# A first norm by channel without transposes, its output kept once

## The chip, the core and the metric

The kernel runs on one core of a Trainium2 chip. The core has five engines that run on their own and wait for each other by semaphores: TensorE (PE; its weight loads are PEld), VectorE (DVE), ScalarE (ACT), GpSimd (POOL) and SyncE (SP), which here only issues DMA transfers. ScalarE and GpSimd issue transfers too. Sixteen DMA engines carry them out. The time is that of the device, in microseconds; a lower one is better.

## What is computed

One layer of a diffusion trunk over 2048 sample tokens and 128 prompt tokens, in float32. Only its beginning matters here:

```python
mod = (jax.nn.silu(cond) @ w_ada + b_ada)[..., None, :]
shift1, scale1, gate1, shift2, scale2, gate2 = jnp.split(mod, 6, axis=-1)
h = rmsnorm(x, g_mix) * (1 + scale1) + shift1
p = h @ w_in
qkv, z, a_raw, b_raw, f = jnp.split(p, IN_SPLITS, axis=-1)
qkv = jax.nn.silu(short_conv(qkv, w_conv)).astype(jnp.float32)
```

`rmsnorm` divides each token's 1024 values by their root mean square. What follows (a delta rule in chunks with triangular inverses, a Fourier group, the output projection, a second norm and a feed-forward part) is the same in both kernels.

## The kernel before

Products of nearly full float32 precision are made of three matmuls: each operand is split into a rounded part `hi` (a ScalarE copy into the matmul's format) and the rest `lo` (a VectorE subtraction), and hi·hi, hi·lo and lo·hi are added in PSUM. The method `split` does this for weights and activations.

The modulation columns come first: `mod_columns(0, ...)` loads 32 pieces of `w_ada`, splits and multiplies them. Beside them `load_halves(wk, 512)` loads and splits the keys' half of `w_in`; eight pieces of its columns for gates and Fourier part, `wfh` and `wfl`, come next.

Then `phase_a` goes over 17 tiles of 128 tokens, the prompt (t = 16) first. A tile is loaded with tokens on partitions; `norm` sums its squares (ScalarE), takes the power -0.5 on GpSimd and scales (ScalarE, `xn`); `norm_T` transposes its eight pieces on TensorE into PSUM and applies scale and shift, half on VectorE, half on ScalarE, into `h` with channels on partitions; two splits make `hi` and `lo`. Both are written to `hT` in DRAM, and 48 matmuls with `wfh` and `wfl` give gates (`ab`) and Fourier input (`f`). Between the tiles, further weights are split and the first block's `hb` loaded.

`qk_pass` then reads `hT` back in eight blocks of 256 tokens (`load_h`, tiles `hb`; the first block has the prompt's 128 columns too), and makes eight projections per block with convolution, activation, products of pairs and, by `fill`, pieces of the triangular inverses. `v_pass` reads all blocks again for values and z.

Each engine executes its instructions in a fixed order, which a scheduler sets when the program is built; the pools of tiles (`bufs`) decide when a load may begin. SyncE's queue issues most loads in one order, so one that waits holds those behind it.

Of the kernel before, what the change touches and what calls it, by code (L numbers as in the profile page):

```python
# [93 lines left out]
class K:  # L94
# [94 lines left out]
    def setup(self):  # L189
# [26 lines left out]
        self.hT = d([2, P, KT, N], F32, name="hT")  # L216
# [139 lines left out]

    def phase_a(self, wk):
# [3 lines left out]
        with ExitStack() as ctx:  # L361
# [8 lines left out]
            qk = self.load_halves(wk, 512)  # L370
            for i, _ in enumerate(self.mod_columns(0, tiles(), "m")):
                if i % 8 == 4:
                    next(qk)
# [7 lines left out]
            qk = chain(qk, self.load_halves(wq, 0))  # L381
            for n, t in enumerate([16] + list(range(16))):
                rows = slice(t * P, (t + 1) * P)
                x = work.tile([P, D], F32, tag="x", name="x")
                nc.sync.dma_start(x, A["x"][rows])
                hi = work.tile([P, KT, P], F32R, tag="hi", name="hi")
                lo = work.tile([P, KT, P], F32R, tag="lo", name="lo")
                self.norm_T(*self.norm(x, 0, work), 0, int(t == 16), hi, lo)
                nc.scalar.dma_start(self.hT[0, :, :, rows], hi.bitcast(F32))
                nc.gpsimd.dma_start(self.hT[1, :, :, rows], lo.bitcast(F32))  # L390
                f = work.tile([P, 512], F32, tag="f", name="f")
                for a, b in ((0, 264), (264, FW)):
                    ps = self.bank("acc")
                    for k in range(KT):
                        self.mm(ps[:, :b - a], hi[:, k], wh[k][:, a:b], start=(k == 0), stop=False)
                        self.mm(ps[:, :b - a], hi[:, k], wl[k][:, a:b], start=False, stop=False)
                        self.mm(ps[:, :b - a], lo[:, k], wh[k][:, a:b], start=False, stop=(k == KT - 1))
                    if a == 0:
                        nc.vector.tensor_copy(self.ab[:, t], ps[:, :16])
# [99 lines left out]
    def load_h(self, n):  # L499
# [10 lines left out]
        tiles = []  # L510
        for k in range(KT):
            if n == 0:
                pair = []
                for l in range(2):
                    t = self.hb.tile([P, BW + NP], F32R, tag="hb", name="hb")
                    nc.sync.dma_start(t.bitcast(F32)[:, :BW], self.hT[l, :, k, start:start + BW])
                    nc.sync.dma_start(t.bitcast(F32)[:, BW:], self.hT[l, :, k, NS:])
                    pair.append(t)
                tiles.append(pair)
                continue  # L520
            t = self.hb.tile([P, 2, BW], F32R, tag="hb", name="hb")
            nc.sync.dma_start(t.bitcast(F32), self.hT[:, :, k, start:start + BW].rearrange("l p t -> p l t"))
            tiles.append((t[:, 0], t[:, 1]))
# [28 lines left out]
    def qk_pass(self, work, wq, wk, ahead):  # L552
        nc, sets, setp = self.nc, self.sets, self.setp
        late = deque()
        for n, b in enumerate(ORDER):
# [17 lines left out]
            for i, (q, h2, which) in enumerate(order):  # L573
# [228 lines left out]
    def v_pass(self, work, wv, wz, ahead):  # L802
# [3 lines left out]
        for n in [7] + list(range(7)):  # L806
# [665 lines left out]
def host_arrays(i):  # L1472
    f = lambda a: np.ascontiguousarray(a)
    a = {k: np.asarray(v) for k, v in i.items()}
    return {
        "x": f(np.concatenate([a["x_sample"][0], a["x_prompt"][0]], 0)),
# [32 lines left out]
```

## Time and profile before

| | |
|---|---|
| median of three runs | 2730.36 us (2729.53 to 2742.19) |
| the profiled execution | 2734.04 us, span 2732.3 us |
| TensorE, its weight loads | 96%, 87% of the span |
| VectorE, ScalarE, GpSimd | 66%, 51%, 11% of the span |
| TensorE's granted clock | 0.982 of full, mean |
| read from memory, written | 294.74 MB, 98.79 MB |

The span runs from the first to the last instruction; busy shares are means over stages with different limits. Lines such as L131 are mostly those of helpers, so instructions are told apart by their tiles: `lo<-h,hi` is the subtraction of a token tile, `w_in<-w_raw,w_in` that of a weight, `hb<-hT` a block's load.

### The profile page before, as it was taken

The numbers are of one execution on the slowest core, as the hardware profiler recorded it, in microseconds if no ns is written. First come the engines' busy times: TensorE is split into PE (matmuls) and PEld (weight loads), VectorE is DVE, ScalarE is ACT, GpSimd is POOL, SyncE is SP. The second block draws the span as 40 slices with busy tenths as digits, with TensorE's granted clock in tenths as the row PEclk, the third lists the DMA queues.
The fourth block names the chain that finished last, engine by engine and source line by source line (L and its number), as shares of the span: only waits on it lengthen the run. The fifth ranks groups of instructions, "written<-read, shape, count | busy, mean of one in ns | idle before, by whom it ended". The sixth has DMA issues, their size and how long they took to land.

```text
span 2732.3 us, 44881 instructions
## 1 busy us (share of the span) xinstructions
PE 2612.4 (96%) x15769; PEld 2374.1 (87%) x15769; DVE 1799.2 (66%) x3916; ACT 1404.5 (51%) x3108; POOL 312.5 (11%) x510
## 2 busy tenths in 40 slices
PE   6999999899999999997999999999999999999998
PEld 3898888799888778876999998889999888999986
DVE  6335978718256676667777766487776557888744
ACT  7756656323378877675333344444334444444432
POOL 1212222222300021211000000020000002000001
PEclk8999999999999999999999999999999999999999
DMA  9957768675666566645222223442222254323242
GB/s 314 307 152 222 222 192 233 185 197 177 159 182 194 174 190 183 184 143 170 78 74 70 74 82 122 140 128 74 73 71 72 88 159 138 90 85 89 90 135 93
DMA packets 436110, 396.50 MB, mean 145 GB/s; under 512 B 123084, under 2 KB 359164, under 8 KB 434284
## 3 DMA queue, kind: packets, MB, share of 16 engines
q1 hardware_dynamic: 345132, 297.65, 36.4%
q0 software_dynamic: 16624, 55.85, 6.2%
q10 hardware_dynamic: 74128, 40.13, 5.2%
q8 instruction: 125, 2.05, 0.3%
q14 instruction: 101, 0.83, 0.1%
HBM read 294.74 MB, written 98.79 MB: 144 GB/s over the span
## 4 chain that ended last, share of the span: by engine, by line
PE 58%; issue 15%; DMA 9%; DVE 8%; ACT 7%; POOL 2%; SPq 1%; ACTq 0%; DVEq 0%; POOLq 0%
PE acc L125 22%; PE m L125 12%; PE acc L1308 12%; PE m L1308 11%; DMA z_s<-z_d 1%; ACT h L141 1%; ACT bd1r L141 1%; PE tr L128 1%; ACT bd0r L141 1%; DMA w_raw<-w_ada 1%; PE tr L125 1%; ACT u L141 1%; DVE inv_d L131 1%; DMA a_d<-la 1%; POOL rstd L131 1%
## 5 line engine op out<-in xcount | busy, mean ns | idle before, releaser
L1308 PE MATMUL m<-h,wh 128*128 128x384 f32 (+1 forms) x1848 | 452.0, 327 | 5.3 <-ACT h L141 2.4
L1308 PE MATMUL acc<-h,wh 128*128 128x384 f32 (+1 forms) x1848 | 450.7, 327 | 2.0 <-ACT wh L141 2.0
L141 ACT ACTIVATE wh<-S 128x512 fp32r<-128x512 f32 x264 | 163.3, 630 | 377.9 <-DVE S L131 151.4
L1308 PEld LDWEIGHTS m<-h,wh 128*128 128x128 f32 x1848 | 327.0, 189 | 7.6 <-DVE U L131 2.9
L1308 PEld LDWEIGHTS acc<-h,wh 128*128 128x128 f32 x1848 | 326.8, 189 | 3.8 <-ACT wh L141 3.3
L125 PE MATMUL acc<-hb,w_in 128*128 128x258 f32 (+1 forms) x2304 | 324.6, 298 | 2.8 <-ACT conv_in L141 2.8
L125 PEld LDWEIGHTS acc<-hb,w_in 128*128 128x128 f32 x2304 | 312.5, 196 | 11.8 <-ACT conv_in L141 3.9
L1308 PE MATMUL acc<-h,wl 128*128 128x384 f32 (+1 forms) x924 | 300.9, 327 | 5.5 <-DVE wl L131 5.5
L1308 PE MATMUL m<-h,wl 128*128 128x384 f32 (+1 forms) x924 | 301.1, 327 | 0.0
L131 DVE TENSOR_TENSOR wl<-S,wh 128x512 fp32r<-128x512 f32 x264 | 178.7, 686 | 7.2 <-ACT wh L141 4.9
L141 ACT ACTIVATE wh<-w_gu 128x512 fp32r<-128x512 f32 x198 | 124.4, 631 | 113.3 <-issue 44.2
L1308 PEld LDWEIGHTS acc<-h,wl 128*128 128x128 f32 x924 | 174.2, 189 | 6.1 <-DVE wl L131 6.1
L1308 PEld LDWEIGHTS m<-h,wl 128*128 128x128 f32 x924 | 173.9, 188 | 0.2 <-DVE wl L131 0.2
L138 DVE SCALAR_TENSOR_TENSOR y<-conv_in,wconv,y 128x256 f32<-128x256 f32 (+1 forms) x216 | 97.7, 466 | 109.3 <-ACT conv_in L141 108.0
L141 ACT ACTIVATE awh<-a 128x384 fp32r<-128x384 f32 x176 | 91.3, 521 | 145.8 <-PE m L125 91.8
L131 DVE TENSOR_TENSOR awl<-a,awh 128x384 fp32r<-128x384 f32 x176 | 97.2, 555 | 97.4 <-ACT awh L141 96.7
L131 DVE TENSOR_TENSOR wl<-w_gu,wh 128x512 fp32r<-128x512 f32 x198 | 135.3, 685 | 24.8 <-ACT wh L141 24.6
L131 DVE TENSOR_TENSOR S<-w_gu 128x512 f32<-128x512 f32 x132 | 91.1, 691 | 84.8 <-DMA w_gu<-w_gu 84.3
L1424 POOL DMA_DIRECT2D half_d<-gy x17 | 9.3, 546 | 1148.6 <-DVE gy L131 1147.4
L138 DVE SCALAR_TENSOR_TENSOR r<-m,nsr,pk 64x128 f32<-64x128 f32 x272 | 94.7, 348 | 49.6 <-PE m L125 45.7
L125 PE MATMUL acc<-woh,mh 128*128 128x512 f32 x272 | 112.2, 413 | 1.5 <-DVE gx L131 1.4
L125 PE MATMUL acc<-wol,mh 128*128 128x512 f32 x272 | 109.3, 402 | 0.0
(295 smaller groups left out, 5780.6 us busy)
## 6 DMA issues: line engine op xcount, KB each, us to landing
w_gu<-w_gu SPq DMA_DIRECT2D x264, 256.0 KB
pk<-pk_d SPq DMA_DIRECT2D x68, 512.0 KB
w_dn<-w_down SPq DMA_DIRECT2D x132, 256.0 KB
hb<-hT SPq DMA_DIRECT2D x104, 258.0 KB
w_raw<-w_ada SPq DMA_DIRECT2D x32, 512.0 KB
x<-x SPq DMA_DIRECT2D x17, 512.0 KB
hT<-hi ACTq DMA_DIRECT2D x17, 512.0 KB
hT<-lo POOLq DMA_DIRECT2D x17, 512.0 KB, 6.1
```

What stands on the lines that cost most here:

```text
L125: self.nc.tensor.matmul(out, lhsT=lhsT, rhs=rhs, start=start, stop=stop)
L128: self.nc.tensor.transpose(out=out, in_=in_, identity=self.c("ident")[:in_.shape[0], :in_.shape[0]])
L131: (eng or self.nc.vector).tensor_tensor(out=out, in0=a, in1=b, op=op)
L138: self.nc.vector.scalar_tensor_tensor(out=out, in0=a, scalar=s, in1=b, op0=op0, op1=op1)
L141: self.nc.scalar.activation(out=out, in_=in_, func=f, **kw)
L1308: nc.tensor.matmul(o, lhsT=w_[:, ws], rhs=h_[:, k, :sub], start=start and k == i == 0, stop=k == 3 and i == 2, skip_group_check=not start)
L1424: nc.gpsimd.dma_start(self.half_d[n], tmp)
```

## The change

The host passes `xT`, x with channels on partitions. A token's sum of squares is now a sum over partitions: ScalarE squares, GpSimd adds the upper four pieces to the lower, VectorE adds twice, and a matmul with a column of ones ends the sum with tokens on partitions. VectorE takes mean and epsilon, GpSimd the power; VectorE puts the factors on a diagonal, a matmul of ones with it repeats them over all partitions, and VectorE multiplies x by that from PSUM. Scale and shift read SBUF. These five stages (`prepare`) run for three tiles at a time. `hT` keeps `h` once, in float32; `load_h` loads it into the tile for `lo`, and `split_h` makes `hi` and `lo` there, a few tiles per projection of the block before. The keys' weights are loaded between the token tiles, not in the modulation stage.

```diff
+    def col_sum(self, work, x):
+        sq = work.tile([P, KT, P], F32, tag="h", name="sq", bufs=3)
+        self.act(sq.rearrange("p k t -> p (k t)"), x.rearrange("p k t -> p (k t)"), AF.Square)
+        self.tt(sq[:, :4], sq[:, :4], sq[:, 4:], ALU.add, eng=self.nc.gpsimd)
+        self.tt(sq[:, :2], sq[:, :2], sq[:, 2:4], ALU.add)
+        total = work.tile([P, P], F32, tag="total", name="total")
+        self.tt(total, sq[:, 0], sq[:, 1], ALU.add)
+        return total
+    def col_factor(self, work, total):
+        ps = self.bank("tr")
+        self.mm(ps[:, 0:1], total, self.c("ones")[:, 0:1])
+        r = self.small.tile([P, 1], F32, tag="rstd", name="rstd", bufs=4)
+        self.ts(r, ps[:, 0:1], 1.0 / D, ALU.mult, EPS, ALU.add)
+        self.rsqrt(r, r)
+        dg = work.tile([P, P], F32, tag="dg", name="dg")
+        self.ts(dg, self.c("ident"), r, ALU.mult)
+        return ps, dg
+    def col_scale(self, x, ps, dg):
+        self.mm(ps[:, P:2 * P], self.c("ones"), dg)
+        self.tt(x, x, ps[:, P:2 * P].unsqueeze(1).to_broadcast([P, KT, P]), ALU.mult)
...
+        self.nc.scalar.dma_start(self.hT[:, :, rows], h)
...
+    def split_h(self, ahead, count):
+        tiles, _, width = ahead
+        for _ in range(count):
+            if self.whole:
+                hi, lo = (x[:, :width] for x in tiles[self.whole.popleft()])
+                self.act(hi, lo.bitcast(F32))
+                self.tt(lo, lo.bitcast(F32), hi.bitcast(F32), ALU.subtract)
...
+            first = {14: [(0, 0)], 18: [(1, 0)], 22: [(0, 1)], 24: [(0, 2), (1, 1)], 26: [(0, 3), (1, 2)], 28: [(1, 3)]}
             for i, _ in enumerate(self.mod_columns(0, tiles(), "m")):
-                if i % 8 == 4:
-                    next(qk)
+                for step in first.get(i, ()):
+                    prepare(*step)
...
-            qk = chain(qk, self.load_halves(wq, 0))
-            for n, t in enumerate([16] + list(range(16))):
+            qk = chain(self.load_halves(wk, 512), self.load_halves(wq, 0))
+            prepare(0, 4)
+            prepare(2, 0)
+            prepare(2, 1)
+            for n, t in enumerate(order):
...
-                self.norm_T(*self.norm(x, 0, work), 0, int(t == 16), hi, lo)
-                nc.scalar.dma_start(self.hT[0, :, :, rows], hi.bitcast(F32))
-                nc.gpsimd.dma_start(self.hT[1, :, :, rows], lo.bitcast(F32))
+                hi, lo = parts.pop(n)
+                prepare(n + 1, 4)
+                prepare(n + 3, 0)
...
+                prepare(n + 2, 3)
+                prepare(n + 3, 1)
-                if n >= 4:
+                if n % 2 == 0:
                     next(qk, None)
                 if n == 8:
                     ahead = self.load_h(0)
+                if n > 10:
+                    self.split_h(ahead, 2)
...
+                if n < 7 and i:
+                    self.split_h(ahead, 1 if i < 7 else 2)
...
+                if n != 6:
+                    self.split_h(ahead, 2)
```

VectorE's order before, up to the fifth token tile, to which `h_905` and `lo_904` belong (`h_813` and `lo_812` are the fourth's; `w_in` and `w_ada` are buffers with weights):

```order
L131 TENSOR_TENSOR w_in_482<-w_raw_1189,w_in_474 128x512
L135 TENSOR_SCALAR h_813<-tr_833,mod_cols_83 128x128 x2
L131 TENSOR_TENSOR w_in_483<-w_raw_1287,w_in_475 128x512
L131 TENSOR_TENSOR w_in_484<-w_raw_1287,w_in_476 128x512
L399 COPY ab_138<-acc_755 128x16
L131 TENSOR_TENSOR w_ada_2352<-w_raw_2351,w_ada_2352 128x512
L131 TENSOR_TENSOR w_ada_2395<-w_raw_2351,w_ada_2395 128x512
L135 TENSOR_SCALAR h_905<-tr_914,mod_cols_83 128x128 x2
L131 TENSOR_TENSOR lo_812<-h_813,hi_811 128x512
L135 TENSOR_SCALAR h_905<-tr_925,mod_cols_83 128x128 x2
L131 TENSOR_TENSOR lo_812<-h_813,hi_811 128x512
L131 TENSOR_TENSOR lo_904<-h_905,hi_903 128x512 x2
```

After the change the fifth tile is `x_677`, `h_843`, `lo_845`. Its `h_843` stands four rows ahead of the first row shown here, behind the scaling of `x_677` and weights of keys and queries; the rows lead to the second half of its `lo_845`:

```order
L131 TENSOR_TENSOR hb_1394<-hb_1394,hb_1393 128x386
L131 TENSOR_TENSOR hb_1398<-hb_1398,hb_1397 128x386
L131 TENSOR_TENSOR x_765<-x_765,tr_887 128x1024
L131 TENSOR_TENSOR hb_1402<-hb_1402,hb_1401 128x386
L131 TENSOR_TENSOR hb_1406<-hb_1406,hb_1405 128x386
L135 TENSOR_SCALAR h_931<-x_765,mod_cols_83 128x128 x4
L131 TENSOR_TENSOR sq_925<-sq_925 128x256
L131 TENSOR_TENSOR hb_1410<-hb_1410,hb_1409 128x386
L131 TENSOR_TENSOR hb_1414<-hb_1414,hb_1413 128x386
L131 TENSOR_TENSOR lo_845<-h_843,hi_844 128x512
L131 TENSOR_TENSOR hb_1418<-hb_1418,hb_1417 128x386
L131 TENSOR_TENSOR lo_845<-h_843,hi_844 128x512
```

Ahead of the fifth tile's `lo` stand now the subtractions of the first block's `hb` and the steps of the sixth tile (`x_765`, `h_931`). The first of the two `lo_845` comes 13 rows after its `h_843`; before, `lo_904` stood two rows behind the last `h_905`.

ScalarE's order after the change where the first block's last projections end; `hb_22..` are the next block's tiles, `conv_in_2658` and `y_2659` the last projection's convolution, `la_2530` products of pairs:

```order
L141 ACTIVATE hb_2207<-hb_2207 128x258
L722 DMA l_d_93<-la_2530 128x4x64
L141 ACTIVATE hb_2209<-hb_2209 128x258
L141 ACTIVATE hb_2211<-hb_2211 128x258
L723 DMA a_d_92<-la_2530 128x8x64
L141 ACT_TABLE_LOAD
L141 ACTIVATE kq_2452<-y_2615 128x4x64
L141 ACTIVATE y_2659<-acc_2633,wconv_86 128x256
L141 ACTIVATE hb_2213<-hb_2213 128x258
L141 ACTIVATE kq_2453<-y_2616 128x2x64
L141 ACTIVATE y_2660<-acc_2633,wconv_86 128x128
L141 ACTIVATE conv_in_2658<-acc_2633 128x386
```

The copies of the next block's loads now stand in this queue, among them and ahead of the last convolution step. Before, no row of ScalarE read `hb`.

## Rows read from the trace of the kernel before

**Rows 1.** The page: busy us of each engine, share of the span, instructions.

```profile
PE 2612.4 (96%) x15769; PEld 2374.1 (87%) x15769; DVE 1799.2 (66%) x3916; ACT 1404.5 (51%) x3108; POOL 312.5 (11%) x510
```

**Rows 2.** Busy time by stretch: length, engines (instructions), PEclk, DMA share, GB/s.

```profile
44.40:61.40 17.00, 12.52 (x84) 12.05 (x84) 11.45 (x24) 13.96 (x31) 3.45 (x6) 0.88 0.95 301
61.40:80.25 18.85, 18.28 (x136) 18.07 (x137) 10.65 (x22) 16.56 (x37) 6.00 (x10) 0.91 1.04 363
80.25:176.90 96.65, 90.46 (x724) 87.10 (x723) 34.09 (x85) 65.86 (x144) 26.61 (x48) 1.00 0.86 265
```

**Rows 3.** The same stretches for the tile `lo` alone.

```profile
44.40:61.40 17.00, 7.05 (x24) 5.00 (x24) 2.74 (x4) 1.97 (x2) 0.88 0.95 301
61.40:80.25 18.85, 11.72 (x40) 8.13 (x40) 4.13 (x6) 2.61 (x3) 0.91 1.04 363
80.25:176.90 96.65, 57.39 (x209) 38.12 (x208) 16.16 (x24) 10.56 (x13) 1.00 0.86 265
```

**Rows 4.** Chain of waits, first 300 us: start us, us, what.

```profile
74.78 11.49 PE acc L125 x92
...
102.06 0.45 PE tr L128 x4
...
106.83 8.28 DMA x<-x
```

**Rows 5.** Busy time by stretch, three blocks of `qk_pass`.

```profile
300.30:332.80 32.50, 32.50 (x310) 29.33 (x310) 31.62 (x102) 23.64 (x46) 9.68 (x9) 1.00 0.71 201
332.80:362.70 29.90, 29.90 (x258) 27.48 (x257) 27.38 (x75) 17.71 (x40) 5.60 (x6) 1.00 0.69 212
...
388.90:436.40 47.50, 41.22 (x398) 36.67 (x399) 27.10 (x63) 21.99 (x50) 14.84 (x22) 0.93 0.81 207
```

**Rows 6.** SyncE's timeline at 223.84 us; chain of waits at 389.70 us.

```profile
223.84 5.60 SPq L522 DMA_DIRECT2D hb<-hT  x10
...
389.70 7.13 DMA hb<-hT
```

**Rows 7.** Groups by shape, 0 to 180 us: busy us, mean ns, idle before.

```profile
L128 PE MATMUL tr<-const_all,xn 128*128 128x128 f32 x136 | 21.2, 290 | 8.9 <-ACT h L141 7.6 <-ACT modv L141 1.2
...
L135 DVE TENSOR_SCALAR h<-tr,mod_cols 128x128 f32<-128x128 f32 x68 | 24.2, 404 | 21.0 <-PE tr L128 17.6 <-ACT h L141 3.2
...
L131 DVE TENSOR_TENSOR lo<-h,hi 128x512 fp32r<-128x512 f32 x34 | 23.0, 687 | 18.7 <-ACT hi L141 18.7
```

**Rows 8.** Timeline of VectorE: start us, us, instruction.

```profile
40.65 0.17 DVE L131 TENSOR_TENSOR mod_cols<-mod_cols,gains 128x16 f32<-128x16 f32 x1
40.93 1.05 DVE L135 TENSOR_SCALAR h<-tr,mod_cols 128x128 f32<-128x128 f32 x3
...
54.92 0.69 DVE L131 TENSOR_TENSOR wfl<-w_raw,wfh 128x528 fp32r<-128x528 f32 x1
...
68.55 1.28 DVE L131 TENSOR_TENSOR w_in<-w_raw,w_in 128x512 fp32r<-128x512 f32 x2
```

**Rows 9.** Groups by shape nearest to the new instructions.

```profile
L131 DVE TENSOR_TENSOR wol<-w_raw,woh 128x1024 fp32r<-128x1024 f32 x4 | 4.9, 1219 | 2.9 <-ACT woh L141 2.9
...
L131 DVE TENSOR_TENSOR ml<-tr,mh 128x256 fp32r<-128x256 f32 x34 | 14.3, 421 | 50.5 <-ACT mh L141 50.4
...
L141 ACT ACTIVATE kq<-y 128x256 f32<-128x256 f32 x64 | 26.2, 416 | 42.5 <-DVE y L138 33.1 <-DVE qs L658 2.9 <-DVE set L131 2.9
...
L131 POOL TENSOR_TENSOR dg<-la,eye 128x256 f32<-128x256 f32 x16 | 11.8, 737 | 31.9 <-DVE la L131 26.1 <-DVE inv_s L135 5.6
...
L131 POOL TENSOR_TENSOR dg<-la,eye 128x128 f32<-128x128 f32 x2 | 0.9, 447 | 7.2 <-DVE la L131 7.2
```

**Rows 10.** Timeline, VectorE and GpSimd side by side.

```profile
344.01 1.51 DVE L131 TENSOR_TENSOR w_ada<-w_raw,w_ada 128x512 fp32r<-128x512 f32 x1
...
344.22 0.74 POOL L131 TENSOR_TENSOR dg<-la,eye 128x256 f32<-128x256 f32 x1
```

**Rows 11.** DMA issues of the page: count, KB each, us to landing.

```profile
hT<-lo POOLq DMA_DIRECT2D x17, 512.0 KB, 6.1
```

More of the change, by code (lines that the diff above doesn't have):

```diff
@@ L215, in setup @@
         d = self.dram.tile
-        self.hT = d([2, P, KT, N], F32, name="hT")
+        self.hT = d([P, KT, N], F32, name="hT")
         self.f_d = d([N, 512], F32, name="f_d")
@@ L355, in load_halves, with col_load @@
             yield
+    def col_load(self, work, t):
+        x = work.tile([P, KT, P], F32, tag="x", name="x", bufs=3)
+        self.nc.sync.dma_start(x, self.A["xT"][t])
+        return x
+    def col_sum(self, work, x):
[6 more added lines that the diff above has]
+        return total
@@ new lines, in mod_split @@
+    def mod_split(self, work, x, t):
+        r, rows = int(t == 16), slice(t * P, (t + 1) * P)
+        h = work.tile([P, KT, P], F32, tag="h", name="h", bufs=3)
+        hi = work.tile([P, KT, P], F32R, tag="hi", name="hi")
+        lo = work.tile([P, KT, P], F32R, tag="lo", name="lo")
+        for g in range(2):
+            for j in range(4):
+                k = g * 4 + j
+                a, b = (self.mod_cols[:, 0, i, k, r:r + 1] for i in range(2))
+                if j < 2:
+                    self.ts(h[:, k], x[:, k], a, ALU.mult, b, ALU.add)
+                else:
+                    self.act(h[:, k], x[:, k], AF.Identity, scale=a, bias=b)
+            ks = slice(g * 4, g * 4 + 4)
+            self.split(hi[:, ks], lo[:, ks], h[:, ks])
+        self.nc.scalar.dma_start(self.hT[:, :, rows], h)
+        return hi, lo
@@ L368, in tiles, with prepare @@
                         yield hi, lo, self.hb.tile([P, 1, 512], F32, tag="hb", name="w_raw")
-            qk = self.load_halves(wk, 512)
+            order = [16] + list(range(16))
+            xs, sums, factors, parts = {}, {}, {}, {}
+            def prepare(n, stage):
+                if n >= NT:
+                    return
+                if stage == 0:
+                    xs[n] = self.col_load(work, order[n])
+                elif stage == 1:
+                    sums[n] = self.col_sum(work, xs[n])
+                elif stage == 2:
+                    factors[n] = self.col_factor(work, sums.pop(n))
+                elif stage == 3:
+                    self.col_scale(xs[n], *factors.pop(n))
+                else:
+                    parts[n] = self.mod_split(work, xs.pop(n), order[n])
+            first = {14: [(0, 0)], 18: [(1, 0)], 22: [(0, 1)], 24: [(0, 2), (1, 1)], 26: [(0, 3), (1, 2)], 28: [(1, 3)]}
             for i, _ in enumerate(self.mod_columns(0, tiles(), "m")):
-                if i % 8 == 4:
-                    next(qk)
+                for step in first.get(i, ()):
+                    prepare(*step)
             wq = self.w_half(0)
@@ L398, in phase_a @@
                     if a == 0:
+                        prepare(n + 2, 2)
                         nc.vector.tensor_copy(self.ab[:, t], ps[:, :16])
@@ L510, in load_h @@
         tiles = []
+        self.whole = deque(range(KT))
         for k in range(KT):
             if n == 0:
[L513 to L523, printed above, removed]
+                hi, lo = (self.hb.tile([P, BW + NP], F32R, tag="hb", name="hb") for _ in range(2))
+                nc.sync.dma_start(lo.bitcast(F32)[:, BW:], self.hT[:, k, NS:])
+            else:
+                t = self.hb.tile([P, 2, BW], F32R, tag="hb", name="hb")
+                hi, lo = t[:, 0], t[:, 1]
+            nc.sync.dma_start(lo.bitcast(F32)[:, :BW], self.hT[:, k, start:start + BW])
+            tiles.append((hi, lo))
         return tiles, segs, width
@@ L1474, in host_arrays @@
     a = {k: np.asarray(v) for k, v in i.items()}
+    x = np.concatenate([a["x_sample"][0], a["x_prompt"][0]], 0)
     return {
-        "x": f(np.concatenate([a["x_sample"][0], a["x_prompt"][0]], 0)),
+        "x": f(x),
+        "xT": f(x.reshape(NT, P, KT, P).transpose(0, 3, 2, 1)),
         "condT": f(np.stack([a["c"][0], a["c_ctx"]], 0).reshape(2, KT, P).transpose(2, 1, 0)),
```

4 lines of the change are left out of this document (removed).

## The prediction

> **What bounds the kernel now.** The page's busy line comes first: TensorE is busy 96% of the span [rows 1], and nothing else passes 87%, so time is won where TensorE waits or where work leaves it. The change touches two stages. The view of busy time by stretch shows the first of them, the token tiles of `phase_a`, from 44.4 to 176.9 us [rows 2]. The same view for the tile `lo` counts its matmuls: 24 and 40 up to 80.25 us, 208 or 209 after it [rows 3]. A token tile has 16 of them, so four tiles are done at 80.25 us and thirteen take the remaining 96.65 us.
>
> What those 96.65 us hold, on TensorE: the chain of waits has 92 projection matmuls in 11.49 us, 0.125 us each, and four transposes in 0.45 us, 0.11 us each [rows 4]. A tile's 48 matmuls are 6.0 us and its eight transposes 0.9 us. The stretch counts 724 matmuls [rows 2]: 13 x 48 = 624, some 80 transposes (ten tiles; the others were transposed earlier) and some 20 of the next stage. That is 78 + 9 + about 3.5 = 90.5 us. About 6 us are waits; one of them is an x tile that lands 8.28 us after its load [rows 4]. So TensorE sets the pace from the fifth tile on, though VectorE is busy only 34 of those 96.65 us and ScalarE 66 [rows 2]. The DMA engines are near full up to 80.25 us (0.95 and 1.04) and 0.86 after it.
>
> The second stage is the eight blocks of `qk_pass`. The view by stretch of three of them [rows 5] shows two kinds: from 300.3 to 362.7 us VectorE is busy 59.0 of 62.4 us, with TensorE just as full; from 388.9 to 436.4 us VectorE is busy 27.1 of 47.5 us, and TensorE 41.2: there loads and their queue order set the pace, one of them an `hb` load of 7.13 us in the chain of waits [rows 6].
>
> **The change, part by part.** *Transposes.* All 136 go [rows 7]. In their place every tile gets two matmuls, of 1 and of 128 columns. The trace of before has no such pair on this path; below, they cost nothing, above, a transpose each, 0.11 us. I take 0.1 us each. From the fifth tile: -9 us and +13 x 0.2 = +2.6, so -6.4 us.
>
> *Moved to VectorE.* Per tile it loses nothing (four `h`, two `lo`, one `ab` stay) and gains five instructions: the sum of squares at 256 and 128 columns, the factor, the diagonal, and x times the factor over 1024 columns. A row's mean is longer than the step from one instruction to the next, as two 512-column subtractions take 1.28 us together where one takes 0.69, and three `h` 1.05 us where one takes 0.40 [rows 7, 8]: steps are 0.60 and 0.33 us. By the nearest rows [rows 9] 1024 columns are 1.2 us, 256 columns 0.34, 128 columns 0.2. The factor and the diagonal, not shown before, lie between a copy's start and an `h`; I take 0.16 and 0.25. So VectorE has, per tile, 2 x 0.6 + 4 x 0.33 + 1.2 + 0.34 + 0.2 + 0.4 + 0.17 = 4.9 us. `h` now reads SBUF in place of PSUM, which could cost as much (0.33) or little over half; I keep 0.33.
>
> *GpSimd's add.* One add of 512 columns per tile is new: 0.45 us at 128 columns, 0.74 at 256 [rows 9], so about 1.3. It holds VectorE up: a subtraction of 0.69 us that was running when such an add began took 1.51 us [rows 10]. The Trainium skill (SBUF — State Buffer, section "SBUF: two separate sides") states this as a lock of the port pair that the two share, held for a whole instruction, when VectorE has two SBUF inputs and GpSimd reads SBUF. This rule speaks against the change: by it each add could hold VectorE for its whole 1.3 us, which makes 6.2 us per tile, while x times the factor reads PSUM and would be free of it; the row agrees with the rule. In rows alone the hold lies between 0 and 1.3 us; I take 0.7, as the stretched subtraction lost 0.8 of an add of 0.74 us, but not every add meets one. VectorE then needs 5.6 us per tile against TensorE's 6.2. TensorE stays the bound from the fifth tile on, narrowly.
>
> *The start.* Here the order matters more than the sums. The keys' weights leave the modulation stage, so the eight `wf` loads follow the last `w_ada` at once; but until the last `wf` split VectorE has 33 instructions, 14.6 us by the steps above, from 40.8 us (the modulation columns are ready [rows 8]). That is 55.4 us; before, the last `wf` subtraction ended at 55.6 us [rows 8]. Nothing is won. (The two tiles prepared before 40.8 us cost VectorE 2 x 2.15 us by the steps, and the eight keys' subtractions that leave this place, at 0.60, are 4.8 us.) Then, in VectorE's order, 54 instructions stand ahead of the fifth tile's second `lo`: 12 weight subtractions (7.3 us), 8 of the first block's `hb` at 386 columns (3.8), 6 `lo` (3.7), 12 `h` (4.0), 3 times x (3.6), and 3 us of small ones: 25.4 us, and 2 us of holds. So the fifth tile is ready at 83 us, where before TensorE began it at 80.25 us: +2.75 us, with TensorE idle for some 10 us after the fourth tile. Bounds: 76 us if `h` costs half and nothing is held; 90 us if the first block's `hb`, which wait for the writes of the first four tiles, land late, because ScalarE and VectorE hold the fifth tile behind them in order.
>
> *Loads.* Half of the writes of hT go (17 of 512 KB on GpSimd's queue [rows 11]) and half of each read. x has three buffers and its loads stand three tiles ahead; of the 6 us of waits I take 3 us as gone. First stage: +2.75 - 6.4 - 3 = about -6.5 us, with bounds of -17 and +7.
>
> *The gates' loads* follow the end of the first stage as before. The next block's `hb` loads are issued at 223.84 us, 47 us after that end [rows 2, 6], behind the decay rows that close the gates' chain. That distance stays; then each tile passes ScalarE and VectorE before TensorE may read it: +0.7 us for the first, the rest beside it.
>
> *Splits in the blocks.* Seven blocks of `qk_pass` issue eight ScalarE copies and eight VectorE subtractions of 258 columns each: 0.42 us each by the 256-column rows of either engine [rows 9], 0.34 us by step, 2.7 us per block and engine. In the stretches of 32.5 and 29.9 us VectorE had 0.9 and 2.5 us free [rows 5], so +1.8 and +0.2 us, and about as much for one further block. In the blocks that wait for loads the cover is the wait itself, and half the bytes shorten it: -1 us each in two, taken low. In `v_pass` TensorE is the bound and the splits lie beside it. Sum of the blocks: +0.7 + 3.3 - 2 = +2 us, bounds -6 and +25.
>
> *Sum.* -6.5 + 2 = -4.5 us. The profiled execution took 2734.0 us for a span of 2732.3; the median of the three runs is 3.7 us lower. 2734.0 - 4.5 - 3.7 = 2725.8; I say **2726 us**.
>
> **The rivals.** *The gain arrives whole.* The fifth tile is ready at 76 us, the waits of the first stage go (-6), the transposes go (-6.4): -16.5 us; and the blocks that wait for loads gain 4 us from the halved `hb`: -20 us, 2710 us. For it: DMA shares of 0.95 to 1.04 at the start [rows 2], and the chain that passes through `hb` loads [rows 6]. Against it: the 54 instructions on VectorE, which no load shortens. It needs VectorE to reach the fifth tile before 79 us.
>
> *Slower: ScalarE waits in order for `hb`.* Before, an `hb` load that landed late held matmuls alone. Now its copy stands in ScalarE's queue between the convolution's steps, which free TensorE's banks, and its subtraction in VectorE's. If a load lands late there, both queues stand, and so does TensorE. For it: the 7.13 us from load to use [rows 6], and ScalarE's order, where the first copies of the next block stand ahead of the current block's last convolution step. Against it: the loads of later blocks are issued most of a block ahead and are half as large. At half of 7.13 us, in seven blocks, it is +25 us: -6.5 + 25 = +18, 2748 us. It ends slower by over 0.5% from 2.9 us a block on.
>
> *No gain at all in the first stage*, because GpSimd's adds hold VectorE for their whole length: VectorE at 6.2 us per tile and the start at 85 us. Then the first stage gains 2 us at most, the blocks take them back, and the time is 2730 us. This lies within the forecast's own range.
>
> **How the numbers follow.** A difference of 0.5%, 13.7 us, is about what can be told from no change here. The forecast, with the third case in it and up to 13.7 us to either side of the median, has a chance of 0.52; the whole gain 0.31; the slower case 0.17. The time given is that of the likeliest. The range for 8 in 10 takes in the fast case beyond its middle and the slow case to its price: 2706 to 2748 us. Faster by over 0.5%: 0.31; within: 0.52; slower: 0.17.
>
> **What would show it.** Right: no transposes of `xn`; TensorE idle for 8 to 12 us before the fifth tile, at 80 to 86 us; 6.2 to 6.6 us per tile after it; the first stage's end at 168 to 172 us; the distance from there to the first matmul of the next block near 52 us; VectorE fuller in the blocks by 2 to 3 us each. Wrong if: the fifth tile starts before 79 us or after 88; the tiles come at VectorE's pace, with gaps before each; ScalarE's `hb` copies show waits on `hb` loads in several blocks; or the stretch from 388.9 to 436.4 us shrinks by much more than 2 us, which would say that its loads were worth more than I took.

## The result, and the profile after

The changed kernel takes 2755.81 us (median of 5 runs, 2751.4 to 2758.14); the kernel before took 2731.94 us in the same comparison. The ratio is 1.0081, with a 95% interval of 1.0063 to 1.0099: slower by 24 us, outside the predicted range (2706 to 2748 us).

The profiled execution has a span of 2754.0 us against 2732.3. Its busy line, to be read beside [rows 1], shows fewer matmuls (68 fewer: 136 transposes gone, 68 small ones come), and yet more busy time on TensorE:

```profile
PE 2619.5 (95%) x15701; PEld 2382.4 (87%) x15701; DVE 1876.4 (68%) x4121; ACT 1425.8 (52%) x3177; POOL 320.9 (12%) x493
```

The view of busy time by stretch of the changed kernel, with the columns of [rows 2]: from the first to the fifth token tile, the thirteen tiles from there, then the eight blocks, the pass over v, and the Fourier and delta stage.

```profile
46.10:84.90 38.80, 30.93 (x208) 29.61 (x208) 31.01 (x67) 27.61 (x57) 10.80 (x12) 0.85 0.94 299
84.90:185.70 100.80, 89.41 (x668) 86.70 (x669) 61.81 (x150) 54.09 (x115) 26.91 (x33) 0.94 0.57 173
185.70:487.30 301.60, 278.66 (x2360) 254.15 (x2360) 240.46 (x642) 190.06 (x422) 72.46 (x89) 0.96 0.63 174
487.30:726.30 239.00, 228.81 (x1446) 203.48 (x1445) 153.61 (x400) 101.94 (x235) 61.63 (x83) 0.94 0.52 143
747.70:950.40 202.70, 190.37 (x1279) 173.65 (x1278) 115.94 (x380) 162.00 (x443) 9.20 (x14) 0.96 0.63 182
```

The same view of the kernel before, for the last three of these stages (the tiles are in [rows 2]):

```profile
176.70:472.60 295.90, 277.59 (x2361) 253.06 (x2359) 221.68 (x581) 172.12 (x363) 69.35 (x89) 0.96 0.69 201
472.60:706.40 233.80, 225.16 (x1446) 202.13 (x1445) 133.60 (x349) 81.24 (x182) 61.83 (x83) 0.95 0.65 182
727.00:925.50 198.50, 186.47 (x1278) 168.52 (x1277) 115.89 (x380) 161.92 (x443) 8.96 (x14) 0.99 0.64 186
```

A row splits its stretch in two: its length less TensorE's busy time is idle time, and busy time that grows while the matmuls don't is a lower granted clock. The thirteen tiles lost 55 instructions and still went from 96.4 to 100.8 us: idle 6.2 to 11.4 us, granted clock 1.00 to 0.94 (a mean over stretches at full, 2.4 GHz, and at half, 1.2 GHz). Behind them the idle time of the blocks went from 18.3 to 22.9 us; the pass over v and the Fourier stage have the matmuls they had and took 3.7 and 3.9 us more busy time for them, at clocks of 0.94 and 0.96 in place of 0.95 and 0.99.

What TensorE waits for among the thirteen tiles is a new pair of rows (us in all, times, longest); before, it waited 5.2 us for `h` ahead of transposes and 0.7 us for `lo`:

```profile
PE acc L125 <- ACT hi L141: 8.9, 7, 3.1
PE acc L125 <- DVE lo L131: 5.7, 6, 1.4
```

The longest of them, 3.1 us, ends where the fifth tile begins and so lies ahead of the stretch. The other 11.5 us are the stretch's idle time: 9.5 us in five places some 15 us apart, 1.5 to 2.6 us each, 1.4 us ahead of the fifth tile's own `lo`, and 0.5 us near the end.

The chain of waits shows one of the five from one end to the other (start us, us, what):

```profile
112.79 3.03 PE acc L125 x24
115.82 0.23 PE tr L125 x2
116.05 0.02 issue
116.08 1.23 DVE x L131
117.31 0.03 issue
117.34 0.66 DVE h L135
118.00 0.04 issue
118.04 0.69 DVE lo L131
118.73 0.04 issue
118.77 0.39 PE acc L125
```

TensorE ends a tile and repeats the factor of the tile after the next (`tr`); VectorE multiplies x by it, begins that tile's `h`, and only then makes the `lo` of the tile that TensorE needs now. ScalarE does the like: by its timeline it squares another tile (1.04 us, at 115.58) before it makes the `hi` needed now, which TensorE gets at 117.19. VectorE's order of the changed kernel shows how this comes: tiles come in pairs, one pair to each of the five places, and the second tile's `x` stands between the first one's `h` and `lo`.

```
L135 TENSOR_SCALAR h_1421<-x_1223,mod_cols_83 128x128 x4
L135 TENSOR_SCALAR dg_1470<-const_all_73,rstd_1467 128x128
L131 TENSOR_TENSOR x_1311<-x_1311,tr_1465 128x1024
L135 TENSOR_SCALAR h_1509<-x_1311,mod_cols_83 128x128 x3
L131 TENSOR_TENSOR lo_1423<-h_1421,hi_1422 128x512
L135 TENSOR_SCALAR h_1509<-x_1311,mod_cols_83 128x128
L131 TENSOR_TENSOR lo_1423<-h_1421,hi_1422 128x512
```

The granted clock of 0.94 comes from three stretches at half; the second row here is one at full, for comparison:

```profile
84.90:91.10 6.20, 4.75 (x20) 4.45 (x21) 6.20 (x14) 6.20 (x14) 0.00 (x0) 0.50 1.03 301
91.10:135.40 44.30, 38.25 (x305) 37.04 (x305) 29.58 (x74) 25.71 (x54) 15.13 (x18) 1.00 0.66 203
135.40:138.90 3.50, 3.50 (x18) 3.50 (x18) 1.98 (x4) 1.58 (x2) 1.25 (x1) 0.51 0.97 299
166.20:169.60 3.40, 3.40 (x18) 3.40 (x17) 2.58 (x6) 1.23 (x3) 0.00 (x0) 0.50 0.75 232
```

A matmul takes 0.125 us in the row at full and 0.19 to 0.24 us in the others. The first stretch at half follows the waits ahead of the fifth tile (1.1 and 3.1 us), the other two follow the third and the fifth pair's waits. Behind the other three pairs' waits the clock did not fall.

### The profile page after: what moved, and what is told of

Read it like the earlier page. It is cut to its first block, busy times and chain, and to the rows that moved or that the text cites. A ratio compares the mean times of both kernels' runs of the same rounds, so it can differ in the third digit from the quotient of the medians.

```text
span 2754.0 us, 45040 instructions
## 1 busy us (share of the span) xinstructions
PE 2619.5 (95%) x15701; PEld 2382.4 (87%) x15701; DVE 1876.4 (68%) x4121; ACT 1425.8 (52%) x3177; POOL 320.9 (12%) x493
## 4 chain that ended last, share of the span: by engine, by line
PE 76%; DVE 7%; ACT 6%; DMA 6%; issue 2%; POOL 1%; SPq 1%; ACTq 0%; DVEq 0%; POOLq 0%
PE acc L125 27%; PE acc L1388 16%; PE m L125 16%; PE m L1388 16%; DMA z_s<-z_d 1%; PE tr L128 1%; PE tr L125 1%; ACT bd1r L141 1%; ACT bd0r L141 1%; ACT h L141 1%; POOL rstd L131 1%; ACT u L141 1%; DMA hb<-hT 1%; DVE y L138 1%; DVE inv_d L131 1%
## 5 line engine op out<-in xcount | busy, mean ns | idle before, releaser
L125 PE MATMUL acc<-hb,w_in 128*128 128x258 f32 (+1 forms) x2304 | 330.9, 299 | 5.9 <-ACT conv_in L141 3.7
L138 DVE SCALAR_TENSOR_TENSOR S<-S,gl,m 128x128 f32<-128x128 f32 x272 | 82.0, 342 | 41.3 <-PE m L125 12.3
```

What stands on the lines that cost most here:

```text
L125: self.nc.tensor.matmul(out, lhsT=lhsT, rhs=rhs, start=start, stop=stop)
L138: self.nc.vector.scalar_tensor_tensor(out=out, in0=a, scalar=s, in1=b, op0=op0, op1=op1)
```

## The experiments

Each row gives the median and the ratio to the kernel before with its 95% interval; then, from the profiled execution, the thirteen tiles from the fifth on (length, TensorE's idle time in it) and the distance from the last token matmul to the program's last matmul ("behind"). Each ratio is to the runs of the kernel before in the same comparison. The stage times are those of one execution each, and the kernel before took 2720.75 to 2742.19 us over all its runs, so a difference of a few us between two kernels in a single stage is not by itself a price.

| kernel | median us | ratio | 13 tiles us (idle) | behind us |
|---|---|---|---|---|
| before | 2731.94 | | 96.4 (6.2) | 2544.0 |
| changed | 2755.81 | 1.0063 to 1.0099 | 100.8 (11.4) | 2557.9 |
| storage alone | 2759.37 | 1.0086 to 1.0122 | 103.3 (8.5) | 2556.9 |
| norm alone | 2766.25 | 1.0108 to 1.0143 | 114.5 (19.1) | 2555.0 |
| add on VectorE | 2735.55 | 1.0011 to 1.0032 | 100.9 (10.9) | 2538.9 |
| own h, one buffer | 2741.93 | 1.0027 to 1.0053 | 98.8 (10.8) | 2540.8 |
| keys back | 2768.13 | 1.0133 to 1.0160 | 106.4 (12.4) | 2560.6 |
| own h, two buffers | 2728.61 | 0.9984 to 1.0004 | 90.0 (5.3) | 2542.0 |
| the same, add on VectorE | 2730.01 | 0.9990 to 1.0016 | 90.7 (4.9) | 2539.1 |
| before, queues swapped | 2750.07 | 1.0067 to 1.0092 | 113.9 (17.2) | 2544.3 |
| norm alone, two buffers | 2747.58 | 1.0039 to 1.0077 | 103.3 (14.4) | 2546.3 |
| two buffers, earlier steps | 2732.16 | 0.9983 to 1.0014 | 89.8 (4.6) | 2543.5 |
| storage alone, three h | 2742.79 | 1.0020 to 1.0056 | 98.3 (5.1) | 2549.6 |

**Storage alone.** The old norm, with the new storage:

```diff
-                self.norm_T(*self.norm(x, 0, work), 0, int(t == 16), hi, lo)
-                nc.scalar.dma_start(self.hT[0, :, :, rows], hi.bitcast(F32))
-                nc.gpsimd.dma_start(self.hT[1, :, :, rows], lo.bitcast(F32))
+                xn, h = self.norm(x, 0, work)
+                self.norm_T(xn, h, 0, int(t == 16), hi, lo)
+                nc.scalar.dma_start(self.hT[:, :, rows], h)
```

> Edit: the kernel before, with its norm by token and its transposes, but hT kept once as float32 and split after its load (load_h and split_h as after). Theory (the first stage's loss of 9 us belongs to the norm, the 13 us lost later belong to the storage): the token tiles end near 177 us as before, the eight blocks take about 3 us more, the pass over v about 5 us more, together 2738 to 2746 us. Rival (the norm's late end moves everything behind it and the storage costs nothing): 2726 to 2732 us, as the loads are half as large.

The blocks took 13.2 us more (295.9 to 309.1), not 3, the pass over v 5 us less, and the first stage, which should have stayed, 10 us more. So the sum behind the first stage (12.9 us) came near the 13 us of the theory from parts that didn't, and the time missed its range. In the sixth of the blocks' intervals TensorE waited 10.1 us for the inverses' loads (2.9 us before); the run with the keys back, below, shows how such a wait comes. The first stage has a wait of its own: ScalarE sat idle ahead of `h` until the write of `hT` landed, 10.0 us in nine places, since the write now reads `h` and holds its buffer.

**Norm alone.** The changed kernel with `hT` in two parts, without `split_h`.

```diff
-        self.nc.scalar.dma_start(self.hT[:, :, rows], h)
+        self.nc.scalar.dma_start(self.hT[0, :, :, rows], hi.bitcast(F32))
+        self.nc.gpsimd.dma_start(self.hT[1, :, :, rows], lo.bitcast(F32))
```

> Edit: the changed kernel, but hT kept in two parts and loaded in two parts, as before; no split_h. Theory: the tiles still come in pairs, so TensorE still waits some 2.6 us for each pair, and the clock still falls in the first stage; without the copies of hb the fifth tile comes 2 to 3 us sooner. First stage ends at 180 to 184 us, the rest is as before: 2736 to 2742 us. Rival (the storage made the whole loss): the first stage ends at or before 177 us and the time is 2730 us or less.

It is slower than the whole change. The thirteen tiles took 114.5 us at a granted clock of 0.90. No copy of `hb` stands ahead of the fifth tile here, and it starts at 84.3 us against 84.9: taking those copies away won 0.6 us. Each part alone loses at least as much as both together, so the loss is not the sum of a price for each.

**The add on VectorE.**

```diff
-        self.tt(sq[:, :4], sq[:, :4], sq[:, 4:], ALU.add, eng=self.nc.gpsimd)
+        self.tt(sq[:, :4], sq[:, :4], sq[:, 4:], ALU.add)
```

> Edit: the changed kernel, with the first add of the squares (512 columns per tile) on VectorE in place of GpSimd. Theory (TensorE waits for an order, not for VectorE's sum of work): VectorE gets 0.6 us more per tile, the waits of each pair remain, the time is 2752 to 2760 us. Rival (GpSimd's add holds VectorE for most of its 1.28 us, and that sets the pace): the tiles speed up by 0.5 us or more each, 7 to 10 us in all, to about 2746 us.

The time fell by 20 us, which the rival foretold better than the theory. But the thirteen tiles, where the hold would have shown, took 100.9 us in place of 100.8. TensorE's waits for `hi` and `lo` fell there from 14.6 to 6.8 us, and one wait of 5.3 us for a sum of squares came up, so this run alone doesn't settle what the hold is worth; the same edit with two buffers, below, does better. The gain lies elsewhere: the fifth tile starts at 80.2 us (84.9), and the stages behind, which have the same operations, take 19 us less.

**Own buffers for h and the squares.**

```diff
-        sq = work.tile([P, KT, P], F32, tag="h", name="sq", bufs=3)
+        sq = work.tile([P, KT, P], F32, tag="sq", name="sq", bufs=2)
...
-        h = work.tile([P, KT, P], F32, tag="h", name="h", bufs=3)
+        h = work.tile([P, KT, P], F32, tag="h", name="h", bufs=1)
```

> Edit: the changed kernel with h in a buffer of its own and the squares in two of their own, in place of three that both share. The scheduler then sets one tile behind the other, no longer in pairs, and in VectorE's order the factor's multiplication of the next tile stands behind the lo of the tile that TensorE needs. Theory (the order in pairs makes the waits): the waits of 2.6 us per pair go, and with them the clock's falls in this stage; the token tiles end at 170 to 176 us and the time is 2738 to 2746 us. Rivals: the hold by GpSimd or the amount of VectorE's work sets the pace: then nothing changes, 2752 to 2758 us; one buffer for h makes each tile wait for the write of the one before: above 2758 us.

Behind the first tiles the pairs went, but the thirteen tiles hardly gained (98.8 us): one tile every 7.3 us, since `h` now waits for the write of the tile before. That is the second rival's mechanism, though not its price (above 2758 us). VectorE's timeline (start us, us, instruction, idle before):

```profile
135.86 1.73 DVE L135 TENSOR_SCALAR h<-x,mod_cols 128x128 f32<-128x128 f32 x4 [1.35 <-DMA hT<-h]
```

**The keys' weights back in the modulation stage.**

```diff
+            qk = self.load_halves(wk, 512)
             for i, _ in enumerate(self.mod_columns(0, tiles(), "m")):
+                if i % 8 == 4:
+                    next(qk)
```

> Edit: the changed kernel, but the keys' weights are loaded and split in the modulation stage, as before. Theory (the fifth tile waits for the work that stands ahead of it in VectorE's and ScalarE's order): twelve to sixteen weight subtractions leave the stretch ahead of the fifth tile, which starts at 78 to 82 us in place of 84.9; the pairs and their waits stay. First stage 3 to 6 us shorter; the stages behind it get another order from the scheduler, which the runs so far moved by up to 10 us either way. Rival (the place of the keys' load is worth nothing, since something else stands there in its place): the fifth tile starts at 84 to 86 us.

Both were wrong: the first tile starts at 51.2 us (46.1) and the fifth at 88.7. With the new steps in the modulation stage, the keys' old place makes the tiles begin 5 us later. In the sixth of the blocks' intervals (411.0 to 466.2 us; 398.1 to 447.8 us in the changed kernel) TensorE waits 10.4 us in two places for the inverses' small loads, `inv_bd`; it waits 3.9 us there in the changed kernel and 2.9 us in one place before. Eight loads of `hb` stand ahead of the small ones in SyncE's queue, but they don't hold them: the last is issued by 413.6 us, and the queue then waits 4.7 us for a write of `xd`, from which the small ones read (rows of SyncE's timeline, of its waits and of TensorE's):

```profile
408.70 4.92 SPq L601 DMA_DIRECT2D hb<-hT  x8
418.45 0.37 SPq L867 DMA_DIRECT2D inv_x<-xd  x1
```

```profile
SPq L867 <- DMA xd<-inv_x: 4.7, 1, 4.7
PE m L125 <- DMA inv_bd<-xd: 10.4, 2, 6.5
```

That write is late because the piece of the inverse in it is made late. ScalarE begins `inv_x` 1.0 us behind the interval's start, and did so 6.7 us ahead of it in the changed kernel (the second fence), where `inv_x` stands ahead of the block's last two convolutions in ScalarE's order; here it stands behind them:

```profile
411.99 2.09 ACT L141 ACTIVATE inv_x<-inv_d 8x1024 f32<-8x1024 f32 x1
```

```profile
391.43 3.18 ACT L141 ACTIVATE inv_x<-inv_d 8x1024 f32<-8x1024 f32 x2 [1.50 <-DVE inv_d L131]
```

**Two buffers for h, one for the squares.** The same space once more:

```diff
-        sq = work.tile([P, KT, P], F32, tag="h", name="sq", bufs=3)
+        sq = work.tile([P, KT, P], F32, tag="sq", name="sq", bufs=1)
...
-        h = work.tile([P, KT, P], F32, tag="h", name="h", bufs=3)
+        h = work.tile([P, KT, P], F32, tag="h", name="h", bufs=2)
```

> Edit: the changed kernel with h in two buffers of its own and the squares in one of their own. Tiles come one behind the other in the scheduler's order, and no tile waits for the write of the tile before it. Theory (pairs make the waits): 6.3 to 6.8 us per tile after the fifth, the waits in that stretch fall from 13.9 to under 8 us, the end of the first stage comes 7 to 11 us after the start that the fifth tile had would give with 7.75 us per tile, so at 174 to 179 us. Rival (VectorE's and ScalarE's work with the hold by GpSimd sets the pace): 7.3 us per tile or more, whatever the order.

The thirteen tiles take 90.0 us, 10.8 less than in the changed kernel, with the same operations. Busy time by stretch of the same four stages, and TensorE's waits in the first of them:

```profile
85.20:175.20 90.00, 84.67 (x666) 81.94 (x667) 61.02 (x152) 54.76 (x119) 29.12 (x35) 1.00 0.63 198
175.20:470.30 295.10, 274.35 (x2360) 250.54 (x2359) 238.91 (x637) 189.56 (x419) 71.00 (x89) 0.98 0.63 176
470.30:699.50 229.20, 221.99 (x1445) 199.78 (x1444) 154.77 (x405) 102.62 (x238) 61.72 (x83) 0.97 0.57 151
721.40:919.40 198.00, 187.72 (x1279) 169.31 (x1277) 116.06 (x380) 161.66 (x444) 9.02 (x14) 0.99 0.63 185
```

```profile
PE acc L125 <- ACT f L141: 2.0, 4, 1.1
PE acc L125 <- ACT hi L141: 1.6, 2, 1.2
PE tr L125 <- DVE ab L474: 1.1, 2, 1.0
PE acc L125 <- DVE lo L131: 0.9, 1, 0.9
```

The waits for `hi` and `lo` in the stretch fell from 11.5 to 2.5 us and the clock stayed full. VectorE is as busy as before the edit (61.0 and 61.8 us), so its sum of work never set the pace. Behind the first few tiles, one tile follows the other in VectorE's order, and `x` stands behind `lo`:

```
L135 TENSOR_SCALAR h_1421<-x_1223,mod_cols_83 128x128 x4
L135 TENSOR_SCALAR dg_1470<-const_all_73,rstd_1467 128x128
L131 TENSOR_TENSOR sq_1503<-sq_1503 128x256
L474 COPY ab_138<-acc_1440 128x16
L131 TENSOR_TENSOR total_1507<-sq_1503 128x128
L131 TENSOR_TENSOR lo_1423<-h_1421,hi_1422 128x512 x2
L131 TENSOR_TENSOR x_1311<-x_1311,tr_1465 128x1024
```

The shared set held work by itself too: in the changed kernel ScalarE's squares waited 3.8 us in four places until a write of `hT` had landed. These waits end 2 to 3 us behind the pairs' waits, so they didn't make those.

**Two buffers, and the add on VectorE.** The buffers as in the run before it, and

```diff
-        self.tt(sq[:, :4], sq[:, :4], sq[:, 4:], ALU.add, eng=self.nc.gpsimd)
+        self.tt(sq[:, :4], sq[:, :4], sq[:, 4:], ALU.add)
```

> Edit: as the run before it, and the add of the squares on VectorE in place of GpSimd. Theory (pairs): no difference to the run before it of more than 3 us in the first stage. Rival (the hold): 0.5 us per tile faster than the run before it.

90.7 us against 90.0: with one tile behind the other, the hold by GpSimd is not what sets the pace.

**The kernel before, with the two writes of hT on each other's queue.**

```diff
-                nc.scalar.dma_start(self.hT[0, :, :, rows], hi.bitcast(F32))
-                nc.gpsimd.dma_start(self.hT[1, :, :, rows], lo.bitcast(F32))
+                nc.gpsimd.dma_start(self.hT[0, :, :, rows], hi.bitcast(F32))
+                nc.scalar.dma_start(self.hT[1, :, :, rows], lo.bitcast(F32))
```

> Edit: the kernel before, with the two writes of hT issued on the other queue each (the first part on GpSimd's, the second on ScalarE's). No work is added or removed; the scheduler sets another order in about a tenth of TensorE's and a sixth of VectorE's places. Theory (a large share of the loss behind the first stage is the order that the scheduler happens to set): stages from the first block on move by 3 to 10 us, either way, and the time is 2722 to 2745 us, not 2731. Rival (the order makes no difference where the work is the same): 2729 to 2733 us, every stage within 2 us of the kernel before.

It lost 20 us with no work added, but not where I looked: behind the first stage it takes 2544.3 us against 2544.0, single stages moving by 4 us at most. All of it lies in the token tiles (113.9 us, 17.2 idle). Nor is the edit neutral: the write of `lo` stands in ScalarE's order and must wait there for VectorE, and ScalarE waited 12.3 us for VectorE's `h` (6.4 before) and 6.7 us in one place until a load of `hb` had landed. By its timeline the instruction held in that place was the issue of the write itself, which came at 106.42 us. The run doesn't show that a new order alone moves the later stages, nor which of these waits made the loss; it shows that an edit of two lines in the old kernel can cost nearly as much as the whole change did.

**Norm alone, with the two buffers.** To the norm alone:

```diff
+        sq = work.tile([P, KT, P], F32, tag="sq", name="sq", bufs=1)
...
+        h = work.tile([P, KT, P], F32, tag="h", name="h", bufs=2)
```

> Edit: the norm alone (hT in two parts, written and loaded as before, no split_h), with h in two buffers of its own and the squares in one of their own. Against the norm alone with shared buffers (2766 us) it shows what the pairs cost there; against the run with both parts of the change and these buffers (2728.6 us) it shows what keeping hT once is worth. Theory: the thirteen tiles after the fifth take 88 to 96 us in place of 114.5, the stages behind them stay within 5 us of the kernel before, 2725 to 2740 us; keeping hT once is then worth less than 5 us either way. Rival (the norm alone is slow because of its second write of hT, whatever the order): the thirteen tiles take 105 us or more.

19 us less than the norm alone with shared buffers, and 19 us more than the whole change with these buffers. The tiles (103.3 us) came between theory and rival; one wait of 6.9 us stands out, in which TensorE needed `f` from ScalarE, which sat idle until loads of `hb` had landed. Again a write of `hT` stood there in ScalarE's order, issued at 114.42 us, and `f` behind it. `hb` in two parts has twice the loads, and they stand between those of x in SyncE's queue until 115.4 us; stored once, they end at 77.6 us. Keeping `hT` once is thus worth something: 13.3 us in the tiles, and 4 us behind them, which are too few to be told from one execution of each.

**Two buffers, steps placed earlier.**

```diff
+            prepare(2, 2)
...
+                prepare(n + 3, 1)
...
-                        prepare(n + 2, 2)
+                        prepare(n + 2, 3)
...
-                prepare(n + 2, 3)
-                prepare(n + 3, 1)
+                prepare(n + 3, 2)
```

> Edit: the changed kernel with h in two buffers of its own, the squares in one of their own, and each step of the norm placed earlier in the program: a tile's sum and factor three tiles ahead, its scaling in the middle of the tile two ahead. Theory (with tiles one behind the other, what is left of TensorE's waits, some 5 us in the thirteen tiles, is the chain of sum, factor and scaling): 1 to 4 us less than with the buffers alone, 2722 to 2730 us. Rival (the scheduler sets its own order and the program's places don't matter): within 2 us of 2728.6 us in the first stage, the rest by the order that comes out.

The same as without the edit: 89.8 us for the tiles; the fifth starts at 83.1 us (85.2), and the rest took that back.

**Storage alone, three buffers for h.**

```diff
-                xn, h = self.norm(x, 0, work)
+                xn, h = self.norm(x, 0, work, 3)
```

> Edit: hT kept once with the norm of before (the storage alone, 2759 us), with three buffers for h in place of two, since h itself is now what the write reads and its buffer stays taken until the write has landed (ScalarE waited 10.0 us for that in nine places of the first stage). Theory: the token tiles end 5 to 10 us sooner, at 177 to 182 us; behind them no work changes, so those stages differ by the order and the clock alone: 2735 to 2755 us, and the storage by itself has no fixed price there. Rival (keeping hT once costs the blocks their time, whatever the order, since ScalarE waits in order for the loads): the stages behind the first take 2555 us or more again, as in the run of the storage alone.

The token tiles end at 181.5 us in place of 186.6, and the stages behind them went from 2556.9 to 2549.6 us with the same operations. That fits the theory, by which the storage has no fixed price there, but 7.3 and 5.6 us (what remains against the kernel before) are too little to be told from one execution of each.

## Why the prediction was wrong

**The step that failed** is "TensorE stays the bound from the fifth tile on, narrowly". It set VectorE's sum of 5.6 us per tile against TensorE's 6.2 and took the smaller one as hidden. VectorE's sum was no larger than that: it was busy 61.8 of 100.8 us, 4.8 us per tile, and still a tile took 7.8 us. The order wasn't looked at: a multiplication that waits for TensorE's end of one tile stood ahead of the subtraction that TensorE's next tile waited for. The two engines waited for each other once per pair of tiles, with TensorE idle for 1.5 to 2.6 us each time. The row that would have said so, `x` between `h` and `lo`, was in VectorE's order before any run. Giving `h` and the squares buffers of their own took most of the pairs away, and with them 6 us of idle time and the falls of the clock in this stretch. This accounts for the tiles alone. Of the 28 us between the forecast (-4.5) and the result (+24), 15.5 lie in the first stage, and some 12 behind it, where the cause stays open.

**The terms of the first stage.** The forecast was -6.5 us; it measured +9.0 (176.7 to 185.7).
- *Start:* forecast 83 us for the fifth tile, measured 84.9. The time was near, the account was not. By the forecast TensorE is idle for some 10 us after the fourth tile; that tile's last matmul ended at 80.1 us, and TensorE was idle for 4.2 us up to the fifth. And the norm alone, without the subtractions of `hb` for which the forecast had 3.8 us, started only 0.6 us sooner.
- *Transposes:* forecast -6.4 us. With two buffers for `h`, at full clock, TensorE is busy 84.7 us in the thirteen tiles against 90.3 before: -5.6. Near.
- *Waits for x:* forecast -3 us. No load of x stands in the chain of waits any more; the waits in order took their place and more, +5.2 us.
- *The clock* had no term. From the fifth tile on it was granted in full before and is 0.94 now: TensorE is busy 89.4 us with 668 matmuls, 84.7 with 666 at full clock, +4.7. About half of that is the stretch at half behind the fifth tile's late start, the other half the two behind pairs' waits. With two buffers for `h` it is 1.00 again; two more kernels with as little idle time there (the same with the add on VectorE, and with earlier steps) have 0.98.

With +4.6 us for the start, these make the 9.0.

**The blocks.** The hop to the first block was forecast at +0.7 us and measured +0.6 (51.6 to 52.2). The +3.3 us for splits in full blocks had the wrong sign: the stretches that answer to the first two of [rows 5] are now 31.3 and 29.1 us, 1.2 and 0.8 shorter (the first with 295 matmuls in place of 310, so it isn't the same work). Of the 3.3 us, the two stretches with rows gave 2.0; the 1.3 for a further block had no row. VectorE is fuller by 18.8 us in the eight blocks, 2.3 each, as foreseen. The -2 us for halved loads in blocks that wait didn't come: the stretch that answers to the last of [rows 5] went from 47.5 to 49.7. The sum is +5.7 against +2.

**The rivals.** *Slower* was right in sign and wrong in place; that its 2748 us came nearer to the result than the forecast did is luck. ScalarE did wait in its order for loads of `hb`, as the waits behind the first stage show:

```profile
ACT hb L141 <- DMA hb<-hT: 29.0, 24, 5.3
```

But TensorE waited for such a copy or its subtraction only 2.1 us in three places there, and with two buffers for `h` ScalarE waits as long (30.0 us) while the time is that of before. The 25 us priced there were never paid. *The hold by GpSimd* is there, but had been taken too large: six of the ten adds in this stretch met an `h` or a `lo`, which lost 0.3 to 0.7 us each, 2.7 us in all, where 0.7 us per tile makes 9. Five of the six lie in the pairs' waits, 2.0 of their 9.5 us. Moving the add changed the tiles by less than 1 us in both orders. *The whole gain* fell with the start.

**Behind the first stage** 13.9 us were lost, of which the forecast had 2. The same 14738 matmuls took 2473.1 us of busy time in place of 2464.9, 8.2 us for the clock, and idle time rose by 5.7. This is not the price of the change's operations: five kernels that hold the whole change and only other buffers, places or engines in the first stage take 2538.9 to 2543.5 us there, no more than the 2544.0 of before, while the one with the keys back takes 2560.6. Two things are shown to move it. One is the order that the scheduler sets, as in the late piece of the inverse with the keys back, 6.5 us of TensorE's wait; in the changed kernel itself that place has only 1.0 us more than before. The other is the clock: in the pass over v, TensorE's orders of the changed kernel and of the storage alone differ in two places; it idles 10.2 and 10.0 us, and is busy 228.8 us in the one (granted clock 0.94) and in the other:

```profile
495.70:724.40 228.70, 218.72 (x1446) 195.12 (x1445) 153.41 (x398) 101.72 (x238) 62.42 (x83) 0.98 0.56 150
```

In the Fourier stage, three kernels with one and the same order on TensorE (add on VectorE, own h with one and with two buffers) take 199.5, 203.3 and 198.0 us, at 0.99, 0.96 and 0.99. What decides in which of these places the clock falls stays open, and so does why the changed kernel falls on the bad side in nearly all: its five runs had clocks of 0.975 to 0.978, so it does so each time.

**The best version** is the change with two buffers for `h`: 2728.6 us, ratio 0.9994 (0.9984 to 1.0004), which can't be told from the kernel before. Its thirteen tiles gain 6.4 us, about what the transposes were worth, and its later start of the fifth tile gives 4.9 of them back.

## What to carry to other kernels

Comparing sums of busy time between two engines says which could be the bound; it doesn't say that the other one is hidden. Where an engine's queue holds an instruction that waits for the bound engine, look at what stands behind it, above all what the bound engine needs next. Buffers that two steps share set the scheduler's order as much as the space: splitting one shared set of three into two and one was worth 10.8 us in the tiles whose order it changed. The whole kernel gained 27 us, but 16 of them lie behind, in stages with the same operations, and why they came is open. A change early in a program that is scheduled as a whole should be measured with two or three orders before a price is put on it.

## What the runs showed of the hardware

GpSimd's add holds more than subtractions. In the kernel with one buffer for `h`, four `h`, which read one tile from SBUF, took 1.73 us (the row above) beside this add, and take 1.12 us in the changed kernel with no such add beside them:

```profile
135.44 1.29 POOL L131 TENSOR_TENSOR sq<-sq 128x512 f32<-128x512 f32 x1 [1.26 <-ACT sq L141]
```

```profile
113.96 1.12 DVE L135 TENSOR_SCALAR h<-x,mod_cols 128x128 f32<-128x128 f32 x4
```

In the changed kernel a single `h` that began at 117.34 us, beside an add from 116.75 to 118.03 us, took 0.78 us and ended 0.09 us behind the add; where no add is near, one takes 0.34 us. It goes the other way too: an add that began at 92.94 us, with a `lo` under way, took 1.80 us in place of 1.28. So what a hold costs depends on how much of the other instruction is left. The prediction's 0.7 us is what a single hold can cost (0.61 here), not a price for each add. The Trainium skill (SBUF — State Buffer, section "SBUF: two separate sides") says that the instruction that starts first keeps the shared ports for its whole length while the other waits, and that on VectorE's side this concerns instructions with two SBUF inputs or in a mode that uses two ports. The times just given agree with the first part; `h` has one tensor from SBUF, and apart from its being held no run here shows its mode. The multiplication of x with a factor from PSUM was never longer than 1.22 us, beside an add or not.
